# Entry of a hybrid retention and attention block: first attention values from x without its norm, and two value groups as seven products of block sums

## The chip, the cores and the metric

The kernel runs on one core of one Trainium2 chip. The metric is the device time of one execution in microseconds (us). Before the change three executions took 2205.68, 2205.74 and 2206.14 us, a median of 2205.74.

The core has a matrix engine (PE, with its weight loads shown apart as PEld), a vector engine (DVE), an activation engine (ACT), a general engine (POOL) and SP, which here only issues transfers. Each works through its own queue in order. ACT and POOL can issue transfers too. Matrix products are accumulated in PSUM (eight banks), which PE writes and DVE and ACT read. Everything else lies in SBUF.

## The reference, cut to what matters

```python
mod = jax.nn.silu(c) @ w_ada[l] + b_ada[l]
sh1, sc1, g1, sh2, sc2, g2 = jnp.split(mod, 6, axis=-1)
h = modulate(rms_norm(x, norm1_g[l]), sh1, sc1)      # rms_norm * (1 + sc1) + sh1
...
proj = h @ w_in
parts = jnp.split(proj, IN_OFFSETS, axis=-1)
...
for gi, (win, dil) in enumerate(ATT_GROUPS):
    aq, ak, av = parts[4 + 3 * gi], parts[5 + 3 * gi], parts[6 + 3 * gi]
```

Sequence and width are 1024. The three attention values `av` are each 1024 x 512 with 1024 summed over. Only they and the making of `h` are touched.

The norm divides a row of x by its root mean square, so each row has one factor (rstd). Writing a for g(1 + sc1), a value row is rstd times (x·a) times W, plus sh1 times W. The last part is the same for every row. This identity is what the change uses.

## The kernel before, in words

All products are float32 results made of two rounded halves: an operand t is split into `hi` (rounded, written by ACT) and `lo` (the rest, written by DVE), and a product is hi·hi + hi·lo + lo·hi, three matmuls. x is held transposed in eight column blocks `xt[k]` of 128 x 1024; `hh[k]` and `hl[k]` are the halves of h.

The entry (`startup`, L401) loads x by rows (`xn`, eight blocks of 512 KB), squares it on ACT for rstd, loads the scale and shift weights `em` and `xt`, and computes the modulation columns on DVE (`mod1`, L458: one multiply with a running sum per 128 columns). `rstd_bcast` spreads rstd over the partitions with four small float32 matmuls for each half. For every k, `h1_mods`, `h1_scale` and `h1_low` make h: DVE multiplies by a and rstd, ACT adds the shift and rounds, DVE forms the low half.

`av_k` (L796) then does values: for group g and column k, 8 row chunks by 3 matmuls of 512 columns into eight PSUM banks. Group 0 follows h column by column (`av_first`); groups 1 and 2 (`av_step`) follow once h is complete. That is 3 groups x 8 x 8 x 3 = 576 matmuls. At the end of a group ACT empties the eight banks and SP writes them to DRAM (`va_d`, L817 and L818). While groups 1 and 2 run, `sums_of_h` prepares the block sums t1, t2 and t3 of h for the next stage, and SP carries the bias rows through DRAM (`bias_out`, L451).

Next comes `queries_keys` (L1007), whose pairs of projections already use seven products of 2 x 2 block sums for eight (`Blocks`), with the same t1 to t4. Its first matmul is the first row named `qap`.

The order of the queues is written out by hand: the program's order is each engine's order. A tile pool has a fixed number of buffers (26 for `x`, three each for `wh` and `wl`), and an instruction that fills one waits for the last reader of what lay there.

Of the kernel before, what the change touches and what calls it, by code (L numbers as in the profile page):

```python
# [11 lines left out]
F32 = mybir.dt.float32  # L12
# [5 lines left out]
P = 128  # L18
D = 1024
# [121 lines left out]
def block_kernel(ctx, tc, io, stop=None, dbg=None):  # L141
# [205 lines left out]
    xt = [x4(f"xt{k}") for k in range(NK)]  # L347
    rb1 = x4("rb1")
# [6 lines left out]
    def early_load(k):  # L355

        for i in (SC1 + k, SH1 + k):
            early[i] = x4(f"em{i}")
            nc.sync.dma_start(early[i], io["w_ada"][i])
        nc.sync.dma_start(xt[k], io["xT"][k])  # L360
# [33 lines left out]
    ss1 = xpool.tile([P, NK], F32, name="ss1")  # L394
    first = {"lows": []}

# [4 lines left out]
    def startup(issue, prepare, limits):  # L401
        limits = iter(limits)
        first["release"] = lambda: issue(next(limits))
        crow, orow = x4("crow")[:1], x4("orow")[:1, :P]
        nc.vector.memset(rel[32:33], 1.0)
        nc.vector.memset(orow, 1.0)
        nc.sync.dma_start(crow, io["c"])

        xn = [x4(f"xn{b}") for b in range(NC)]
        for b in range(NC):  # L410
            nc.sync.dma_start(xn[b], io["x"][b])
            if b == 1:
                nc.sync.dma_start(rel[:32], io["rel_bias"])
                for g in range(3):
                    nc.sync.dma_start(bias_cut(onehot, g)[:33], io["onehot"][:, 384 * g:384 * g + 384])
            if b == 4:
                nc.sync.dma_start(ct, io["cst"])
                nc.sync.dma_start(vec, io["vec"])
        for k in range(NK):
            early_load(k)  # L420
            if k in (0, 1, 3):
                issue((k + 3) // 2)
        for j in range(2):
            pc = ps_s(f"pc{j}")
            nc.tensor.matmul(pc, orow, crow[:, j * 512:(j + 1) * 512], start=True, stop=True)
            nc.scalar.activation(cb[:, j * 512:(j + 1) * 512], pc, AF.Silu)
        for b in range(NC):
            nc.scalar.activation(xn[b], xn[b], AF.Square, accum_out=ss1[:, b:b + 1])
        for g in range(3):
            bias_rows(g)  # L430
        rs = rstd_of(ss1, "n1", xpool)
        mod1(0)
        nc.vector.tensor_scalar_add(bs1, vec[:, VC_BADA + SC1:VC_BADA + SC1 + NK], 1.0)
        h1_mods(0)
        first["rb"] = [rstd_bcast(rs, 4 * j, 4, f"n1{j}") for j in range(2)]
        prepare(1)
        for j in range(2):
            h1_scale(0, j)
        mod1(1, (SC1,))
        h1_low(0)  # L440
        first["lows"].pop(0)()
        mod1(1, (SH1,))
# [32 lines left out]

    def h1_mods(k):
        sh = mods[:, SH1 + k:SH1 + k + 1]
        nc.vector.tensor_add(sh, sh, vec[:, VC_BADA + SH1 + k:VC_BADA + SH1 + k + 1])
        nc.vector.scalar_tensor_tensor(a1[:, k:k + 1], mods[:, SC1 + k:SC1 + k + 1], bs1[:, k:k + 1],
                                       vec[:, VC_N1 + k:VC_N1 + k + 1], op0=ALU.add, op1=ALU.mult)  # L480

    def h1_scale(k, j=None):

        ts = slice(0, S) if j is None else slice(512 * j, 512 * j + 512)
        t = xt[k][:, ts]
        nc.vector.scalar_tensor_tensor(t, t, a1[:, k:k + 1], rb1 if j is None else first["rb"][j],
                                       op0=ALU.mult, op1=ALU.mult)
        nc.scalar.activation(hh[k][:, ts], t, AF.Identity, bias=mods[:, SH1 + k:SH1 + k + 1])

    def h1_low(k):  # L490
        nc.vector.scalar_tensor_tensor(hl[k], xt[k], mods[:, SH1 + k:SH1 + k + 1], fv(hh[k]),
                                       op0=ALU.add, op1=ALU.subtract)
# [301 lines left out]
    av = {}  # L794

    def av_k(g, k, w):  # L796

        ws = slice((k % 2) * 512, (k % 2) * 512 + 512)
        if k == 0:
            av[g] = [ps_s(f"av{g}{c}") for c in range(NC)]  # L800
        if g == 0:

            parts = ((hh, 0), (hl, 0), (hh, 1)) if k == 0 else ((hh, 1), (hh, 0), (hl, 0))
            groups = (parts[:1], parts[1:2], parts[2:]) if k == 0 else (parts[:2], parts[2:])
        else:
            parts = ((hh, 1), (hh, 0), (hl, 0))
            groups = (parts,)
        for group in groups:
            for c in range(NC):
                for x, j in group:  # L810
                    nc.tensor.matmul(av[g][c], x[k][:, c * C:(c + 1) * C], w[j][:, ws], start=k == 0 and (x, j) == parts[0],
                                     stop=k == NK - 1 and (x, j) == parts[2], skip_group_check=True)
        for c in range(NC) if k == NK - 1 else ():
            if c % 2 == 0:
                t = x4(f"avo{g}{c}")
            o = t[:, DV * (c % 2):DV * (c % 2) + DV]
            nc.scalar.copy(o, av[g][c])  # L817
            nc.sync.dma_start(va_d[g][c * C:(c + 1) * C], o)  # L818

    def split_first(raw):  # L820
        hi = whl.tile([P, 1024], F32R, tag="wh", name=raw.name + "h")
        lo = whl.tile([P, 1024], F32R, tag="wl", name=raw.name + "l")
        nc.scalar.copy(hi, raw)
        first["lows"].append(lambda: nc.vector.tensor_sub(lo, raw, fv(hi)))
        return hi, lo

    split_first.weight = True

    def av_first(kk):

        def body(ahead, w):
            for k in (2 * kk, 2 * kk + 1):
                if k == 0:
                    for j, rb in enumerate(first["rb"]):
                        nc.scalar.copy(rb1[:, 512 * j:512 * j + 512], rb)
                if k % 2 == 0:
                    ahead(1)
                if k + 1 < NK:
                    h1_mods(k + 1)
                    h1_scale(k + 1)  # L840

                    if first["lows"]:
                        first["lows"].pop(0)()
                        h1_low(k + 1)
                        if k + 2 < NK:
                            mod1(k + 2)
                    elif k + 2 < NK:
                        mod1(k + 2, (SC1,))
                        h1_low(k + 1)
                        mod1(k + 2, (SH1,))  # L850
                    else:
                        h1_low(k + 1)
                av_k(0, k, w)
                if k == 3:
                    first["release"]()
                if k == 4:
                    for g in range(3):
                        bias_out(g)
                if k == NK - 1:
                    ahead(1)  # L860
                    if first["lows"]:
                        first["lows"].pop(0)()
                    nc.sync.dma_start(cs, io["cossin"])
                    nc.sync.dma_start(decay, io["decay"])
        return body
# [8 lines left out]
    def sums_of_h(name, ms=range(4)):  # L874

        low = None
        for m in ms:
# [4 lines left out]
            if name == "t1":  # L882
                r = e0
                nc.vector.tensor_sub(r, e0, e1)
            elif name == "t3":
                r = e1
                nc.vector.scalar_tensor_tensor(r, e1, dsh1[:, m:m + 1], o1, op0=ALU.add, op1=ALU.subtract)
            elif name == "t2":
                r = o1
                nc.vector.scalar_tensor_tensor(r, o1, sh, e0, op0=ALU.add, op1=ALU.add)  # L890
            else:
                r = o0
                nc.vector.scalar_tensor_tensor(r, o0, sh, o1, op0=ALU.add, op1=ALU.subtract)
# [3 lines left out]
            if low:  # L897
                nc.vector.tensor_sub(low[0], low[1], fv(low[2]))
            hi, lo = XA[name, m]
            nc.scalar.copy(hi, r)  # L900
            low = lo, r, hi
        nc.vector.tensor_sub(low[0], low[1], fv(low[2]))

    def av_step(g, kk):
        def body(w):
            if (g, kk) == (1, 0):
                for m in range(4):
                    nc.sync.dma_start(h12_d[m][:, 0], fv(hh[2 * m][:, 512:]))
                    nc.sync.dma_start(h12_d[m][:, 1], fv(hl[2 * m][:, 512:]))
                sh = mods[:, SH1:SH1 + NK].rearrange("p (m j) -> p m j", j=2)  # L910
                nc.vector.tensor_sub(dsh1, sh[:, :, 0], sh[:, :, 1])
            for k in (2 * kk, 2 * kk + 1):
                av_k(g, k, w)
            if g == 1 and kk < 3:
                sums_of_h(("t1", "t3", "t2")[kk])
# [1665 lines left out]
```

## Time and profile before

| what | value |
|---|---|
| median of three runs | 2205.74 us |
| span of the profiled execution, first to last instruction | 2203.6 us |
| around the span, by the median | 2.1 us |
| PE busy in the span | 2170.7 us (99%) |
| DVE, ACT, POOL busy | 1456.9, 922.9, 160.6 us |
| DRAM read, written | 316.27 MB, 156.13 MB |

The profiled execution has no time of its own beside its span. A row of the timeline reads: start, duration, engine, line of the code, operation, result and operands, and in brackets the idle time before it with what ended it. `128x512` is partitions by elements. A row of the groups has the busy time of the group and the mean of one instruction in ns after the bar. PE rows overlap, because matmuls are pipelined: the rate is the distance from start to start.

### The profile page before, as it was taken

What the parts mean: (1) busy time and instruction counts of PE and PEld (TensorE: products, weight loads), DVE (VectorE), ACT (ScalarE), POOL (GpSimd) and SP (SyncE); (2) the same over time, 40 slices, a digit from 0 to 9 for tenths busy, and PEclk for the clock granted to TensorE, in tenths of its full rate; (3) what the DMA queues carried; (4) which work ended last, traced back from release to release, by engine and by line L of the source; (5) the groups of instructions that cost most, each with busy time, mean ns of one, the idle gap of its engine ahead of it and who ended that gap; (6) DMA issues with size and microseconds to landing.
All of it is one profiled execution on the core that took longest, in us unless ns stands there. A gap on an engine that the chain in (4) does not pass through costs nothing. (4 is left out here: it accounts for less than half of the span.)

```text
span 2203.6 us, 27246 instructions
## 1 busy us (share of the span) xinstructions
PE 2170.7 (99%) x10134; PEld 1802.4 (82%) x10134; DVE 1456.9 (66%) x2284; ACT 922.9 (42%) x1691; POOL 160.6 (7%) x192
## 2 busy tenths in 40 slices
PE   7999999999999999999999999999999999999998
PEld 4888888888887888888888888888778888888887
DVE  6618777763547778865564754677876665887855
ACT  4323332223334445444554634524455445533413
POOL 0001111000011122111100000001100000000003
PEclk9999999999999999999999999999999999999999
DMA  9539999634676556557863265654144344745322
GB/s 367 202 128 284 304 289 292 193 115 172 233 267 209 166 179 220 177 161 197 195 173 97 87 244 186 239 179 160 62 166 152 146 149 177 262 136 175 119 86 77
DMA packets 156611, 408.93 MB, mean 186 GB/s; under 512 B 27446, under 2 KB 55357, under 8 KB 153278
## 3 DMA queue, kind: packets, MB, share of 16 engines
q1 hardware_dynamic: 148542, 363.14, 46.8%
q0 software_dynamic: 7936, 44.05, 9.2%
q8 instruction: 80, 1.31, 0.2%
q14 instruction: 53, 0.43, 0.1%
HBM read 316.27 MB, written 156.13 MB: 214 GB/s over the span
## 5 line engine op out<-in xcount | busy, mean ns | idle before, releaser
L207 PE MATMUL qap<-hh,qaw 128*128 128x512 f32 x216 | 84.0, 389 | 0.0
L209 PE MATMUL qap<-hl,qaw 128*128 128x512 f32 x216 | 84.0, 389 | 0.0
L211 PE MATMUL qap<-hh,qaw 128*128 128x512 f32 x216 | 84.0, 389 | 0.0
L638 POOL TENSOR_TENSOR j<-qk,j 128x512 fp32r<-128x512 f32 x32 | 43.3, 1353 | 458.3 <-ACT j L637 441.7
L1902 POOL TENSOR_TENSOR accnf<-accnf,sqnf 128x256 f32<-128x256 f32 (+1 forms) x18 | 16.6, 922 | 609.6 <-ACT sqnf L1898 609.6
L2006 ACT ACTIVATE a<-a 128x512 f32<-128x512 f32 x48 | 30.3, 631 | 73.3 <-DVE a L2005 73.3
L1322 ACT ACTIVATE P<-P,ng 128x128 f32<-128x128 f32 (+1 forms) x96 | 42.0, 439 | 37.5 <-DVE ng L1319 37.5
L264 DVE TENSOR_TENSOR qaw<-wa,qaw 128x512 fp32r<-128x512 f32 x54 | 36.0, 685 | 30.4 <-ACT qaw L254 30.4
L2214 ACT CAST w2h<-w2s 128x512 fp32r<-128x512 f32 x36 | 22.4, 622 | 80.0 <-DVE w2s L2252 78.8
L264 DVE TENSOR_TENSOR fw<-w1r,fw 128x512 fp32r<-128x512 f32 x48 | 32.9, 688 | 33.6 <-ACT fw L254 33.6
L207 PE MATMUL fp<-h2h,fw 128*128 128x512 f32 x128 | 50.0, 391 | 0.0
L211 PE MATMUL fp<-h2h,fw 128*128 128x512 f32 x128 | 49.8, 389 | 0.0
L209 PE MATMUL fp<-h2l,fw 128*128 128x512 f32 x128 | 49.8, 389 | 0.0
L207 PE MATMUL roa<-rh,rwl 128*128 128x512 f32 x128 | 49.8, 389 | 0.0
L209 PE MATMUL roa<-rl,rwh 128*128 128x512 f32 x128 | 49.8, 389 | 0.0
L211 PE MATMUL roa<-rh,rwh 128*128 128x512 f32 x128 | 49.8, 389 | 0.0
L1737 DVE TENSOR_TENSOR rwl<-rwl,rwh 128x1024 fp32r<-128x1024 f32 x25 | 30.2, 1221 | 29.0 <-ACT rwh L1767 29.0
L673 ACT COPY sm<-sT 128x128 f32<-128x128 f32 x32 | 8.5, 267 | 93.8 <-PE sT L661 93.8
L207 PEld LDWEIGHTS qap<-hh,qaw 128*128 128x128 f32 x216 | 40.6, 188 | 8.5
L211 PEld LDWEIGHTS qap<-hh,qaw 128*128 128x128 f32 x216 | 40.6, 188 | 8.4
L209 PEld LDWEIGHTS qap<-hl,qaw 128*128 128x128 f32 x216 | 40.6, 188 | 8.4
L1902 POOL TENSOR_TENSOR accn<-accn,sqn 128x512 f32<-128x512 f32 x12 | 15.5, 1293 | 392.2 <-ACT sqn L1898 392.2
(3104 smaller groups left out, 7211.6 us busy)
## 6 DMA issues: line engine op xcount, KB each, us to landing
v<-vd SPq DMA_DIRECT2D x32, 512.0 KB, 5.0
raw<-in_w_ada_dram SPq DMA_DIRECT2D x32, 512.0 KB, 5.0
w1r<-in_w_ff_dram SPq DMA_DIRECT2D x32, 512.0 KB, 4.8
vd<-vo SPq DMA_DIRECT2D x24, 512.0 KB, 6.4
yt<-y POOLq DMA_DIRECT2D x24, 512.0 KB, 6.9
xsd<-as SPq DMA_DIRECT2D x24, 512.0 KB, 2.7
w2r<-in_w_ff2s_dram SPq DMA_DIRECT2D x24, 512.0 KB, 7.2
em<-in_w_ada_dram SPq DMA_DIRECT2D x16, 512.0 KB, 10.2
```

The costliest lines, as they stand in the source:

```text
L207: nc.tensor.matmul(o, wl, xh, start=first, stop=False, skip_group_check=skip)
L209: nc.tensor.matmul(o, wh, xl, start=False, stop=False, skip_group_check=skip)
L211: nc.tensor.matmul(o, wh, xh, start=False, stop=last, skip_group_check=skip)
L264: nc.vector.tensor_sub(t[:, 512:], src, fv(t[:, :512]))
L638: nc.gpsimd.tensor_sub(t[:, 1], src, fv(t[:, 0]))
L673: nc.scalar.copy(sm, ps[:, :C])
L1322: nc.scalar.activation(v, v, AF.Exp, bias=ng[:, blk:blk + 1], accum_out=st[:, g, blk, 2 + a:3 + a])
L1737: nc.vector.tensor_sub(lo, fv(lo), fv(hi))
L1902: (nc.vector if f == 7 else nc.gpsimd).tensor_add(G["acc", key], G["acc", key], sq)
L2006: nc.scalar.activation(o, o, AF.Relu)
L2214: nc.scalar.copy(hi, src)
```

## The change

Four things are exchanged:

- **Group 0 without rstd and shift.** The products run on x·a, split without the norm (`plain_split`, `plain_low`). rstd is computed on the side, stored to DRAM (`rs_d`) and read back in two layouts: spread over all partitions (`rb1`) and one factor for each row (`rsn`). ACT multiplies by `rsn` when it empties a bank. The shift's part is made by POOL from the raw weights (`shift_rows`, `shift_sum`), summed over the partitions by two float32 matmuls with ones (`shift_out`), and added to `va_d[0]` in DRAM by four accumulating transfers.
- **h later.** `h_scale` and `h_split` make the true h from `xt` after the plain products, half by half, where the seven products need it.
- **Groups 1 and 2 as seven products.** Their 1024 x 1024 weight lies as blocks in DRAM (`w_av2`). `UPLAN` names the seven products, each 4 row chunks x 4 x 3 = 48 matmuls of 512 columns. POOL adds the weight blocks (`u_sum`), ACT and DVE split them (`u_w`), and `u_post` adds the seven results.
- **Loads.** `c` is read spread over the partitions in place of a matmul; small tables go through the queues of ACT and POOL. The order of loads is one list, drawn by `more`. The low halves of the group 0 weights 1 to 3 and of the first product move from DVE to POOL.

The diff, cut to its core:

```diff
+    def plain_split(k, ts):
+        nc.scalar.mul(hh[k][:, ts], xt[k][:, ts], a1[:, k:k + 1])
+    def plain_low(k):
+        nc.vector.scalar_tensor_tensor(hl[k], xt[k], a1[:, k:k + 1], fv(hh[k]), op0=ALU.mult, op1=ALU.subtract)
+    def h_scale(k, j):
+        t = xt[k][:, 512 * j:512 * j + 512]
+        nc.vector.scalar_tensor_tensor(t, t, a1[:, k:k + 1], rb1[0][:, 512 * j:512 * j + 512],
+                                       op0=ALU.mult, op1=ALU.mult)
+    def h_split(k, j):
+        ts, sh = slice(512 * j, 512 * j + 512), mods[:, SH1 + k:SH1 + k + 1]
+        t, hi, lo = xt[k][:, ts], hh[k][:, ts], hl[k][:, ts]
+        nc.scalar.activation(hi, t, AF.Identity, bias=sh)
+        late_low(lambda: nc.vector.scalar_tensor_tensor(lo, t, sh, fv(hi), op0=ALU.add, op1=ALU.subtract))
...
+    def wa_split(kk, parts=(slice(0, 1024),)):
...
+            nc.scalar.copy(hi[:, cs_], raw[:, cs_])
+            if kk > 0:
+                nc.gpsimd.tensor_sub(lo[:, cs_], raw[:, cs_], fv(hi[:, cs_]))
...
+            if k == 5:
+                rs = rstd_of(ss1, "n1", xpool)
+                rb1.append(x4("rb1"))
+                nc.gpsimd.dma_start(rs_d.rearrange("o (p b) -> (o p) b", b=NC), rs)
+                nc.gpsimd.dma_start(rb1[0], rs_d.to_broadcast([P, S]))
+                for j in (0, 4):
+                    src = bass.AP(tensor=rs_d.tensor, offset=rs_d.offset + P * j, ap=[[1, P], [P, 4]])
+                    nc.gpsimd.dma_start(rsn[:, j:j + 4], src)
+            if k + 1 < NK:
+                scale_mod(k + 1)
+                for ts in (H0, H1):
+                    plain_split(k + 1, ts)
+                if k % 2 == 1:
+                    wa_split((k + 1) // 2)
+                plain_low(k + 1)
...
+            if k == 6:
+                for m in range(4):
+                    h_scale(2 * m, 0)
+                    h_split(2 * m, 0)
+                u_w(0, 0, "pool")
+                u_w(0, 1, "pool")
+                late_low()
+        for c in range(NC):
+            mms(NK - 1, [(hh, 1), (hh, 0), (hl, 0)], [c])
...
+            nc.scalar.mul(o, av[c], rsn[:, c:c + 1])
+            nc.sync.dma_start(va_d[0][c * C:(c + 1) * C], o)
...
+    UPLAN = {"11": ("11", 1, "a"), "12": ("21", 1, "b"), "s1": ("t1", 1, "c"), "s2": ("t2", -1, "a"),
+             "s4": ("22", 1, "c"), "s3": ("t3", -1, "a"), "22": ("t4", -1, "a")}
...
+    def more_values(ahead):
...
+            if i == 0:
+                u_load(1)
+            if n == "11":
+                u_w(1, 0)
+                u_w(1, 1)
+                for m in range(4):
+                    u_mm(0, 0, [m])
+                    u_mm(0, 1, [m])
+                    u_mm(0, 2, [m])
+                    u_mm(0, 3, [m])
+                    for k in range(2 * m + 1, 2 * m + 2):
+                        shift_mod(k)
+                        h_scale(k, 0)
+                        h_split(k, 0)
+                        shift_rows(k - 1)
+                late_low()
+                u_load(2)
...
+                for m in range(4):
+                    h_scale(2 * m, 1)
+                u_sum(2)
+                for k in (1, 3, 5, 7):
+                    shift_rows(k)
+                for kk in (1, 2, 3):
+                    shift_sum(kk)
+                for g in range(3):
+                    bias_out(g)
+                continue
+            for p in range(4):
+                u_mm(i, p)
+                if post:
+                    u_post(*post.pop())
+                post.append((i, p))
+                if p == 0 and n[0] != "2" and USEQ[i + 1][0] == "s" and i > 1:
+                    u_sum(i + 1)
+                if p == 1 and i + 2 <= last:
+                    u_load(i + 2)
+                if n == "12":
+                    sums_of_h("t1", [p])
+                    if p > 1:
+                        u_w(2, p - 2)
...
+                elif n == "s3":
+                    sums_of_h("t4", [p])
+                    if p > 1:
+                        u_w(6, p - 2)
+                    if p == 3:
+                        late_low()
+                        shift_out()
```

In the parts left out, product `s1` is accompanied by t2 and the weights of `s2`, `s2` by the second halves of h (`h_split`) and the weights of `s4`, and `s4` by t3 and the weights of `s3`. `late_low` holds back one low half, so that it is formed behind the next instruction's start. The fourth sum t4, made within `queries_keys` before, is made in `s3`.

More of the change, by code (lines that the diff above doesn't have):

```diff
@@ L419, in startup @@
[L419 to L442, printed above, removed]
+    def late_low(f=None):
+        if first["lows"]:
+            first["lows"].pop()()
+        if f:
+            first["lows"].append(f)
@@ L820, in split_first @@
[L820 to L865, printed above, removed]
@@ new lines, in u_load @@
+    def u_load(i):
+        n = USEQ[i]
+        for j in range(2):
+            if n in ("s1", "s3"):
+                U["sum", n == "s3", j] = t = x4(f"usum{i}{j}")
+                u_raw(t, "21", j)
+        for j in range(2):
+            if i == 0:
+                U["more", i, j] = x4(f"uraw{j}")
+            else:
+                U["more", i, j] = whl.tile([P, 1024], F32, tag=("wh", "wl")[j], name=f"um{i}{j}")
+            u_raw(U["more", i, j], {"s1": "22", "s2": "11", "s4": "12", "s3": "11"}.get(n, n), j)
@@ new lines, in shift_rows, with shift_sum, shift_out @@
+    def shift_rows(k):
+        t = wa[k // 2][0][:, 512 * (k % 2):512 * (k % 2) + 512]
+        nc.gpsimd.tensor_scalar_mul(t, t, mods[:, SH1 + k:SH1 + k + 1])
+    def shift_sum(kk):
+        nc.gpsimd.tensor_add(wa[0][0], wa[0][0], wa[kk][0])
+    def shift_out():
+        ps = ps_s("shw")
+        for j in range(2):
+            nc.tensor.matmul(ps, ones.to_broadcast([P, P]), wa[0][0][:, 512 * j:512 * j + 512], start=j == 0, stop=j == 1)
+        t = x4("shw")
+        for j in range(2):
+            nc.scalar.copy(t[:, 512 * j:512 * j + 512], ps)
+        for i in range(4):
+            dst = va_d[0][2 * C * i:2 * C * (i + 1)].rearrange("(a p) x -> p a x", p=P)
+            nc.gpsimd.dma_start(dst, t.rearrange("p (a x) -> p a x", a=2), accum_op=ALU.add)
@@ L1154, in values @@
         banks(False)
-    for kk in range(4):
-        steps.add(av_first(kk), [(io["w_av"][kk], split_first)], manual=True)
-    for g in (1, 2):
-        for kk in range(4):
-            steps.add(av_step(g, kk), [(io["w_av"][4 * g + kk], split_first if (g, kk) == (1, 0) else split_w)])
-    steps.mark()
+    steps.add(first_values, manual=True)
+    steps.add(more_values, manual=True)
     steps.add(queries_keys, manual=True)
```

292 lines of the change are left out of this document (202 added, 90 removed).

## The prediction

> **What bounds the kernel now.** I read the page's totals first, then the waits of PE in the first 320 us, then three windows cut where the stages change, then the timeline at the cuts.
>
> ```profile
> span 2203.6 us, 27246 instructions
> PE 2170.7 (99%) x10134; PEld 1802.4 (82%) x10134; DVE 1456.9 (66%) x2284; ACT 922.9 (42%) x1691; POOL 160.6 (7%) x192
> ...
> PE n10rb L387 <- POOL n1rs L380: 8.6, 1, 8.6
> PE av L811 <- ACT hh L488: 3.5, 5, 1.2
> ...
> 0.00:23.17 23.17, 11.40 (x26) 5.32 (x26) 3.88 (x11) 14.08 (x24) 2.78 (x5) 1.00 0.92 350
> 23.17:74.80 51.63, 48.01 (x203) 37.62 (x203) 43.66 (x63) 17.25 (x22) 0.00 (x0) 1.00 0.75 282
> 74.80:159.60 84.80, 84.80 (x375) 70.23 (x375) 28.44 (x39) 25.50 (x38) 0.00 (x0) 1.00 0.45 161
> ...
> 149.64 0.39 PE L811 MATMUL av<-raw_880h,hh 128*128 128x512 f32 x1
> ...
> 159.39 0.39 PE L811 MATMUL av<-raw_880h,hl 128*128 128x512 f32 x1
> 159.62 0.39 PE L207 MATMUL qap<-hh,qaw 128*128 128x512 f32 x1
> ```
>
> PE sets the time: 99% busy, with no wait behind the entry. The entry waits for rstd (8.6 us) and for h (3.5 us), and the first value product starts at 23.17 us. In the third window PE never rests, while DVE is busy for 28.44 of 84.80 us (columns: length, then busy PE, PEld, DVE, ACT, POOL) and POOL not at all. The 43 steps from 149.64 to 159.39 give 0.227 us per matmul. The first `qap` at 159.62 us is my mark: behind it PE is full, so whatever the mark moves by, the end moves by.
>
> **What the change takes from PE.** Seven products are 7 x 48 = 336 matmuls against 384 for two groups: 48 x 0.227 = 10.9 us less. `shift_out` adds two plain float32 products of 512 columns:
>
> ```profile
> 21.38 1.91 PE L387 MATMUL n11rb<-ct,n1rs 128*128 128x128 f32 x8
> ```
>
> Four products of 128 columns (eight records) took 1.9 us, so two of 512 cost 3.6 us. Group 0 can start near 11 us, 12 us sooner, since it waits for c, one scale block, one x block and half a weight, not for all of x. If PE never waited, 63 us for the end of group 0, 336 matmuls (76.3) and 3.6 would put the mark near 143 us, 16.7 us early. The question is what feeds PE.
>
> **What the change loads on DVE and POOL.** Durations, and how these two meet:
>
> ```profile
> L463 DVE SCALAR_TENSOR_TENSOR em<-em,cb 128x1024 f32<-128x1024 f32 x16 | 19.3, 1220 | 0.0
> 33.96 1.22 DVE L463 SCALAR_TENSOR_TENSOR em<-em,cb 128x1024 f32<-128x1024 f32 x1
> 35.22 0.16 DVE L478 TENSOR_TENSOR mods<-mods,vec 128x1 f32<-128x1 f32 x1
> 35.30 0.21 DVE L479 SCALAR_TENSOR_TENSOR a<-mods,bs,vec 128x1 f32<-128x1 f32 x1
> 162.57 1.41 DVE L893 SCALAR_TENSOR_TENSOR xt<-xt,mods 128x512 f32<-128x512 f32 x2
> 676.59 1.29 DVE L764 TENSOR_TENSOR statel<-state,stateh 128x512 fp32r<-128x512 f32 x2
> L1902 POOL TENSOR_TENSOR accn<-accn,sqn 128x512 f32<-128x512 f32 x12 | 15.5, 1293 | 392.2 <-ACT sqn L1898 392.2
> L1902 POOL TENSOR_TENSOR accnf<-accnf,sqnf 128x256 f32<-128x256 f32 x12 | 8.8, 737 | 15.4 <-ACT sqnf L1898 15.4
> ...
> 639.72 1.29 POOL L638 TENSOR_TENSOR j<-qk,j 128x512 fp32r<-128x512 f32 x1 [0.30 <-ACT j L637]
> 639.77 2.31 DVE L1072 TENSOR_TENSOR vwl<-vwl,vwh 128x1024 fp32r<-128x1024 f32 x1
> 1485.33 1.29 POOL L1902 TENSOR_TENSOR accn<-accn,sqn 128x512 f32<-128x512 f32 x1 [342.84 <-ACT sqn L1898]
> 1486.23 1.48 DVE L198 TENSOR_TENSOR raw_12332l<-raw,raw_12332h 128x1024 fp32r<-128x1024 f32 x1 [1.64 <-ACT raw_12332h L197]
> 2157.18 1.29 POOL L1902 TENSOR_TENSOR accnf<-accnf,sqnf 128x512 f32<-128x512 f32 x1 [2.62 <-ACT sqnf L1898]
> 2157.21 0.75 DVE L2369 SCALAR_TENSOR_TENSOR x1r<-f2l,mods,x1r 128x512 f32<-128x512 f32 x1 [0.84 <-PE f2l L211]
> ```
>
> From start to start DVE needs 1.15 us for 1024 columns, 0.7 for the three-operand form of 512 and 0.64 for the plain one; a modulation column with its addition costs 1.3 (33.96 to 35.30). POOL's two sizes differ by 0.55 us per 256 columns, so 1024 columns should take 2.4 us.
>
> The pairs of rows at 639 and 1485 us matter most. A DVE operation that alone takes 1.2 us took 2.31 and ended at 642.08, which is 1.07 behind POOL's end at 641.01; the other ended at 1487.71, 1.09 behind POOL's 1486.62. DVE stood still until POOL was done. Both its operands lay in SBUF. At 2157.21 one operand (`f2l`) lay in PSUM, and DVE ran at its usual 0.75 beside POOL. So I count POOL's time onto DVE's wherever DVE reads two SBUF operands.
>
> All collisions in this trace are of the plain two-operand form. About 35 us of DVE's new work behind group 0 (counted below) is the three-operand form, which shift columns, scales, low halves of h and three of the sums use. The nearest row says that the place of the operands decides, so I take it to collide as well; the bounds are no collision and the whole of POOL's time.
>
> The Trainium skill's page "SBUF — State Buffer", section "Who interferes with whom", states this generally: a DVE instruction with two SBUF inputs shares a read interface with any POOL instruction that reads SBUF, and the second to start waits for the first to end. By that rule the three-operand form collides too and the sum stays as below; by the plain form alone it would be the second rival's.
>
> **The chain, step by step.**
>
> ```profile
> 12.86 1.06 ACT L428 ACTIVATE xn<-xn 128x1024 f32<-128x1024 f32 x1 [0.84 <-DMA xn<-in_x_dram]
> 14.15 1.06 ACT L428 ACTIVATE xn<-xn 128x1024 f32<-128x1024 f32 x1
> 22.40 0.72 ACT L488 ACTIVATE hh<-xt,mods 128x512 fp32r<-128x512 f32 x1 [0.79 <-DVE xt L486]
> 25.69 1.05 ACT L823 CAST raw_315h<-raw 128x1024 fp32r<-128x1024 f32 x1
> 71.19 4.01 ACT L817 COPY avo<-av 128x512 f32<-128x512 f32 x8 [4.41 <-PE av L811]
> 75.23 6.70 SPq L818 DMA_DIRECT2D vad<-avo  x8
> raw<-in_w_ada_dram SPq DMA_DIRECT2D x32, 512.0 KB, 5.0
> L380 POOL TENSOR_TENSOR n1rs<-n1rs,ct 128x8 f32<-128x8 f32 x1 | 2.6, 2572 | 16.4 <-DVE n1rs L379 16.4
> 651.11 0.54 POOL L1145 DMA_DIRECT2D hl<-h12d  x1 [4.88 <-issue]
> ```
>
> *To the end of group 0.* A block of 512 KB lands every 1.3 us (12.86, 14.15; the former is x's sixth, so the first lands by 6.4). Column 7's x is the 29th in the new list: 43 us. Scale column, two ACT pieces (0.72 each) and low half add 4.1; with POOL's weight difference in the way DVE is through column 7 at about 48.5. Four shift columns (5.2), four scales and four lows (5.6) and the collision with POOL's third weight difference (2.4) bring it to 61.7. That difference stands in POOL's queue behind the power (2.6), three issues of the rstd transfers and their wait; the small-element read of `rsn` is unknown, between nothing and the 4.9 us that one transfer waited at 651.11. It can hold PE before column 6, so group 0 ends between 63 and 67. This is cover: nothing below hangs on it, since DVE is later.
>
> *The gate.* ACT's queue has the halves of h, then the first product's two weight casts (2 x 1.05), then the eight evictions (4.0): it empties the first bank at 63 and the last at 67. SP's eight stores last 6.7 us as before, to 70.3, and only behind them does SP issue the load of the second product's weights. Landing (5.0) and cast (1.05) make 76.4. In DVE's queue that weight's low half stands ahead of the four odd shift columns and all that follows, so DVE idles from 62 to 76, though nothing else keeps it. POOL's first low halves and even shift rows fall into that gap and cost nothing.
>
> *From 76.4 on DVE and POOL in a row.* DVE: product `11`: two weight lows 2.3, four shift columns 5.2, four scales and four lows 5.6, four more scales 2.8 = 15.9. `12`: t1 (8 x 0.64), two weight lows 2.3, three posts 2.1, four scales 2.8 = 12.3. `s1`: 8.4 (a post, t2, weight lows). `s2`: eight lows, four sums, weight lows 10.7. `s4`: three posts, t3, weight lows 9.8. Together 57.1. POOL: four `u_sum` of two adds 19.2; odd shift rows 4 x 0.9 (one operand; between half and all of the 1.29 above) 3.6; three `shift_sum` 7.2. Together 30.0. The seven posts read PSUM and could run beside POOL (4.9); I credit half, 2.5. The last low half for `s3` is then made at 76.4 + 57.1 + 30.0 - 2.5 = 161.0.
>
> PE needs only 44 us for `12` to `s4`, so it waits at every stage; the first wait, in the first row chunk of `12`, is over 10 us by itself (PE is through `11` near 77, the last odd low half comes near 95). Behind 161.0 PE has most of `s3` (9.3), `shift_out` (3.6) and `22` (10.9): mark at **184.8 instead of 159.6, 25 us later**. The span becomes 2228.8. The median lies 2.1 us above the span now, and I keep that: **2231 us**, 1.1% slower.
>
> The remaining edits go together at nothing: t4 moved out of the queries stage, `a_load` moved behind the values, the bias rows on SP and the copy of h to DRAM. All are covered by PE's full queue there; the bias rows occupy SP some 19 us, and the next weights are needed later than that:
>
> ```profile
> 55.40 0.39 SPq L453 DMA_DIRECT2D browd<-rows  x1
> ...
> 71.85 2.39 SPq L456 DMA_DIRECT2D biasd<-browd  x4
> ```
>
> **The rivals.**
>
> *No collision to speak of (not slower).* If DVE runs its three-operand forms freely and POOL takes the gaps, only the gate at 76.4 and PE remain: `12`'s first chunk ends 13.1 + 0.7 later at 90.2, then 8.2 for its rest, five products (54.5), 3.6 and some 3 us of late weight lows: mark at 159.6, time 2206. It decides from the point where less than a tenth of POOL's 30 us reaches DVE. With stores as fast as the evictions the gate is 2.7 earlier: 2203. For it speaks that no three-operand collision is in this trace; against it the two pairs of rows.
>
> *Half a collision.* Only plain forms wait, or POOL finds DVE waiting for ACT half the time: 15 us less, 2216.
>
> *More waits.* The rstd transfers (4-byte pieces on POOL's queue) or tile buffers hold the evictions by 7 us, and POOL's eleven additions take 3.0 us each, 6.6 more: 2245. The 4.88 us wait speaks for it.
>
> *The start does not move:* if the plain products began no sooner than 23 us, DVE would be 12 us later throughout: 2243. The order of loads speaks against it.
>
> **How the numbers follow.** Forecast (2222 to 2240) 0.50; half a collision 0.19; more waits 0.12; the start 0.02; no collision 0.17. A run of this kernel tells 0.2%, 4.4 us, from no change: 2201.3 to 2210.2 is the same. No collision is split between same and faster, since gate and evictions can be some us earlier: faster 0.08, same 0.09, and slower 0.83 for the rest. The range 2205 to 2247 leaves out the faster part of no collision and the far end of more waits.
>
> **What would show it.** Right: first `av` product near 11 us; DVE idle for over 10 us ahead of the second product's weight low; PE waiting for DVE in `12`, `s1`, `s2` and `s3`; DVE rows of the three-operand form at 512 columns lasting 2 to 3 us beside POOL rows of 2.4; the first `qap` near 185. Wrong: such rows at 0.75 beside POOL, or a PE without waits behind 95 us.

## The result, and the profile after

Four executions of the changed kernel took 2233.91 to 2236.72 us, a median of 2235.55; four of the kernel before beside them had a median of 2205.84. The ratio is 1.0135, with a 95% interval of 1.0120 to 1.0149: about 30 us slower. The profiled execution took 2236.72 us with a span of 2234.9, 31.3 above the span before.

The page's totals:

```profile
span 2234.9 us, 27298 instructions
PE 2172.3 (97%) x10070; PEld 1799.1 (80%) x10070; DVE 1508.1 (67%) x2320; ACT 939.6 (42%) x1720; POOL 226.6 (10%) x225
```

PE's waits in the first 260 us (us in all, times, longest):

```profile
PE av L847 <- POOL wv3wl L801: 12.9, 1, 12.9
PE ub L207 <- DVE hl L438: 10.4, 3, 7.8
...
PE uc L209 <- DVE uwl L939: 4.9, 4, 2.4
PE qap L207 <- DVE qat L293: 3.8, 1, 3.8
PE uc L207 <- ACT uwh L934: 3.5, 1, 3.5
```

And the line of the instructions on `qap` whose first start I had taken as the mark (shortest, median and longest ns, then first and last start):

```profile
L207 PE MATMUL qap<-hh,qaw x216: 389/389/795, 184.3 to 530.5; 128*128 128x512 f32 x108
```

The mark lies at 184.3 us, 24.7 later than before. The span grew by 31.3, so 6.6 us were lost behind the mark.

The entry in the windows that answer to those of before (length, then busy PE, PEld, DVE, ACT, POOL with their instructions, then the granted clock, the DMA share and GB/s), with one window behind the mark:

```profile
23.17:74.80 51.63, 38.76 (x161) 31.52 (x160) 31.30 (x42) 26.62 (x42) 21.05 (x13) 0.87 0.72 282
74.80:160.00 85.20, 64.17 (x236) 48.59 (x235) 77.65 (x80) 30.25 (x47) 41.99 (x17) 0.84 0.52 180
...
220.00:230.00 10.00, 8.68 (x28) 6.95 (x29) 9.71 (x16) 3.28 (x6) 0.52 (x1) 0.68 0.72 204
```

In the third window DVE went from 28.44 to 77.65 us of about 85, POOL from nothing to 41.99, and PE, which was full, issued 236 matmuls up to 160.00 where it had issued 375 up to 159.60. The clock fell too, which it had not done before.

The places in the timeline that carry the chain, in order of time:

```profile
11.96 3.78 PE L847 MATMUL av<-wv0wh,hh 128*128 128x512 f32 x8 [1.36 <-ACT hh L412]
...
57.47 0.77 POOL L861 DMA_DIRECT2D rsn<-rsd  x1 [6.96 <-issue]
58.23 2.94 DVE L438 SCALAR_TENSOR_TENSOR hl<-xt,mods,hh 128x512 fp32r<-128x512 f32 x1
58.25 2.35 POOL L801 TENSOR_TENSOR wv3wl<-wv,wv3wh 128x1024 fp32r<-128x1024 f32 x1
60.66 0.79 PE L847 MATMUL av<-wv3wl,hh 128*128 128x512 f32 x1 [12.87 <-POOL wv3wl L801]
61.75 0.74 DVE L438 SCALAR_TENSOR_TENSOR hl<-xt,mods,hh 128x512 fp32r<-128x512 f32 x1
...
69.54 5.45 ACT L893 ACTIVATE avo<-av,rsn 128x512 f32<-128x512 f32 x8 [2.40 <-PE av L847]
70.26 5.08 SPq L894 DMA_DIRECT2D vad<-avo  x8
74.10 0.39 PE L207 MATMUL ua<-uwh,hl 128*128 128x512 f32 x1
75.44 1.99 SPq L906 DMA_DIRECT2D um<-in_w_av_dram  x2
80.07 1.06 ACT L934 ACTIVATE uwh<-um 128x1024 fp32r<-128x1024 f32 x1 [5.07 <-DMA um<-in_w_av_dram]
81.22 1.23 DVE L939 TENSOR_TENSOR uwl<-um,uwh 128x1024 fp32r<-128x1024 f32 x1 [12.00 <-ACT uwh L934]
...
99.92 9.13 DVE L430 SCALAR_TENSOR_TENSOR xt<-xt,a,rb 128x512 f32<-128x512 f32 x4
100.22 8.27 POOL L983 TENSOR_TENSOR wv<-wv,wv 128x1024 f32<-128x1024 f32 x3
...
116.44 2.75 POOL L926 TENSOR_TENSOR usum<-usum,um 128x1024 f32<-128x1024 f32 x1 [7.94 <-DVE uwl L939]
116.88 3.40 DVE L939 TENSOR_TENSOR uwl<-usum,uwh 128x1024 fp32r<-128x1024 f32 x1
...
160.96 1.23 DVE L941 SCALAR_TENSOR_TENSOR uwl<-usum,uwh 128x1024 fp32r<-128x1024 f32 x1
```

The same DVE form lasts 2.94 us at 58.23 and 0.74 at 61.75; beside the first stands a POOL operation that ends at 60.60. Four scales take 9.13 us beside three POOL additions. DVE waits 12.00 us for the second product's weight, whose load SP issues at 75.44, behind eight stores that wait for the evictions, which wait for PE, which waited 12.87 us for a POOL operation behind the transfers of rstd. The first `ua`, at 74.10, is the first matmul behind group 0.

What was lost behind the mark, POOL's and ACT's timeline:

```profile
175.05 1.29 POOL L995 DMA_DIRECT2D vad<-shw  x1 [31.00 <-ACT shw L992]
181.45 1.23 POOL L995 DMA_DIRECT2D vad<-shw  x1 [5.11 <-issue]
187.94 1.21 POOL L995 DMA_DIRECT2D vad<-shw  x1 [5.25 <-issue]
202.73 1.19 POOL L995 DMA_DIRECT2D vad<-shw  x1 [13.59 <-issue]
...
210.37 0.62 ACT L254 CAST qaw1s<-qas 128x512 fp32r<-128x512 f32 x1 [8.39 <-DMA vad<-shw]
211.93 0.58 ACT L286 COPY qat<-qap 128x512 f32<-128x512 f32 x1
...
221.32 0.80 PE L207 MATMUL qap<-hh,qaw 128*128 128x512 f32 x1 [3.82 <-DVE qat L293]
```

The four accumulating transfers of the shift read a tile of the `x` ring and go out slowly. The cast of a later weight into that ring waits 8.39 us for them, and behind it in ACT's queue stands the copy `qat` that PE needs. PE stands for 3.8 us, and then its clock is 0.68 over 10 us, which is worth up to another 3.2 (an estimate: 0.32 of 10 us).

### The profile page after: what moved, and what is told of

It reads as the page before. It is cut to its first block, busy times and chain, and to the rows that moved or that the text cites. A ratio compares the mean times of both kernels' runs of the same rounds, so it can differ in the third digit from the quotient of the medians.

```text
span 2234.9 us, 27298 instructions
## 1 busy us (share of the span) xinstructions
PE 2172.3 (97%) x10070; PEld 1799.1 (80%) x10070; DVE 1508.1 (67%) x2320; ACT 939.6 (42%) x1720; POOL 226.6 (10%) x225
## 5 line engine op out<-in xcount | busy, mean ns | idle before, releaser
L2199 ACT ACTIVATE a<-a 128x512 f32<-128x512 f32 x48 | 30.3, 631 | 73.6 <-DVE a L2198 73.6
L207 PEld LDWEIGHTS qap<-hh,qaw 128*128 128x128 f32 x216 | 41.1, 190 | 12.9 <-DVE qat L293 4.2
L2200 ACT ACTIVATE a<-a 128x512 f32<-128x512 f32 x64 | 40.5, 632 | 2.0
```

The source lines that it names most:

```text
L207: nc.tensor.matmul(o, wl, xh, start=first, stop=False, skip_group_check=skip)
L2199: nc.scalar.activation(o, o, AF.Relu)
L2200: nc.scalar.activation(o, o, AF.Square)
```

## The experiments

My theory: one chain (late third weight, late evictions, late load, then DVE and POOL in a row) sets the mark, and a DVE operation with two SBUF operands stands still while POOL reads SBUF. The rivals: POOL's work lies in gaps; PE's own late end of group 0 decides; or one of the two waits alone.

Each experiment below except the last pair has one run and one trace. Five kernels that are equal up to the gate (DVE's first row for the second product's weight: the changed one, `pool_add`, `pool_set`, `sums_dve`, `shw_tile`) have it between 80.65 and 82.40 us, so a single difference of marks is good to one or two microseconds.

### Does POOL's time count onto DVE's?

Three additions into a tile that nobody reads any more, behind the shift sums on POOL; and in their place fills of the same tile, which read nothing:

```diff
                     shift_sum(kk)
+                for _ in range(3):                              # pool_add
+                    nc.gpsimd.tensor_add(wa[1][0], wa[2][0], wa[3][0])
+                for _ in range(6):                              # pool_set, instead
+                    nc.gpsimd.memset(wa[1][0], 0.0)
```

> Three more additions of 128 x 1024 on POOL behind the shift sums, over weights that nobody reads any more: 8.3 us of POOL time, placed where POOL idles until 116 us. Theory (the collision): DVE loses nearly all of it, first qap 6 to 8 us later at 190 to 192, time 2241 to 2244. Rival (POOL matters only through what it hands on): nothing waits for these, 184 and 2235.

> At the place of the three extra additions POOL runs six fills of 128 x 1024, which write SBUF and read nothing. Theory (DVE's second SBUF operand and POOL's reads share one way in): no collision, first qap at 184 to 185, time 2235 to 2236. Rival (any POOL instruction stops DVE): the fills' own time, some 3 to 8 us, is lost as with the additions, 187 to 192, time 2239 to 2243.

With the additions the first `qap` came at 192.5 and the run took 2243.88 us: 8.2 later, beside 8.32 us more of POOL. POOL and DVE there:

```profile
109.01 8.32 POOL L1031 TENSOR_TENSOR wv<-wv,wv 128x1024 f32<-128x1024 f32 x3
...
109.53 2.86 DVE L1108 TENSOR_TENSOR xt<-xt 128x512 f32<-128x512 f32 x1
112.31 0.67 DVE L972 TENSOR_TENSOR ur<-ur,ub 128x512 f32<-128x512 f32 x1
112.90 2.23 DVE L1108 TENSOR_TENSOR xt<-xt 128x512 f32<-128x512 f32 x1
115.06 2.83 DVE L1125 TENSOR_TENSOR xat<-xt,xat 128x512 fp32r<-128x512 f32 x1
```

With the fills it came at 183.6 (2235.09 us), no later than in the changed kernel:

```profile
107.87 5.99 POOL L1031 MEMSET wv<- 128x1024 f32 x6
...
108.40 0.68 DVE L1108 TENSOR_TENSOR xt<-xt 128x512 f32<-128x512 f32 x1
109.00 0.67 DVE L972 TENSOR_TENSOR ur<-ur,ub 128x512 f32<-128x512 f32 x1
```

The near match of 8.2 and 8.32 is in part chance. The gate had come 0.57 us later before any addition ran (81.79 for 81.22). The three stretched rows are 5.9 us longer than the 0.68 that they take alone, and 1.8 us more came later, where DVE waited for PE (1.65 us at 163.43). So an addition cost DVE itself about 2 us of its 2.8.

So it is POOL's reading that stops DVE, not that POOL is busy; and `ur`, whose second operand lies in PSUM, keeps its 0.67 us beside an addition too. The Trainium skill's page "SBUF — State Buffer", section "Who interferes with whom", says just this: a DVE instruction with two SBUF inputs contends with a POOL instruction that reads SBUF, not with one that only writes. The two runs agree on each half of it.

### POOL's work taken away

All eight additions of weight blocks go to DVE, which then has more to do:

```diff
-            nc.gpsimd.tensor_add(s, s, U["more", i, j])
+            nc.vector.tensor_add(s, s, U["more", i, j])
```

> The eight additions of weight blocks move from POOL (2.6 to 2.8 us each) to DVE (1.15 each). Theory: POOL's eight cost DVE some 17 us by standing still, its own eight cost 9.2, so first qap some 6 to 9 us earlier at 175 to 178, time 2226 to 2229, though DVE has more to do. Rival (DVE is bound by its own work, POOL runs beside it): 9 us later, 193, time 2244.

The first `qap` came at 176.9 and the run took 2227.35 us: 7.4 earlier, though DVE makes eight operations more and the gate, which the edit does not touch, came 1.2 us later (82.40). Next, the shift rows and sums left out:

```diff
-                        shift_rows(k - 1)
...
-                for k in (1, 3, 5, 7):
-                    shift_rows(k)
-                for kk in (1, 2, 3):
-                    shift_sum(kk)
```

> The eight shift_rows and three shift_sum on POOL are left out, so the shift's part of the group 0 values is not the reference's. Nothing on PE or DVE waits for them before s3. Theory (DVE stands still while POOL reads): the odd rows and the sums lay over a dense DVE from 91 to 108 us, so 12 to 17 us go: first qap at 168 to 172, time 2218 to 2223. Rival (no collision: DVE's own work and the late load bound): under 2 us, 2233 to 2235.

It came at 177.4 (2228.84 us), 6.9 earlier and not 12 to 16. The scales that stood beside the sums went from 9.13 us back to 2.73:

```profile
98.70 2.73 DVE L430 SCALAR_TENSOR_TENSOR xt<-xt,a,rb 128x512 f32<-128x512 f32 x4
```

That is 6.4 of the 6.9. The rows (one operand, 1.55 us each when alone) had run beside short DVE operations and cost little: 6.9 less 6.4 leaves 0.5. My price for the sums (7.2) was about right, the one for the rows (3.6) too high.

### The waits ahead

The second product's load ahead of the eight stores; the odd shift columns ahead of its weight lows in DVE's queue; the reads of rstd from DRAM moved in POOL's queue behind the third weight's difference:

```diff
             nc.scalar.mul(o, av[c], rsn[:, c:c + 1])          # load_first
-            nc.sync.dma_start(va_d[0][c * C:(c + 1) * C], o)
+            outs.append(o)
+        u_load(1)
+        for c, o in enumerate(outs):
+            nc.sync.dma_start(va_d[0][c * C:(c + 1) * C], o)
...
             if n == "11":                                     # odd_first
-                u_w(1, 0)
-                u_w(1, 1)
                 for m in range(4):
...
                         shift_rows(k - 1)
+                u_w(1, 0)
+                u_w(1, 1)
                 late_low()
...
-                nc.gpsimd.dma_start(rb1[0], rs_d.to_broadcast([P, S]))   # wv3_early
-                for j in (0, 4):
-                    src = bass.AP(tensor=rs_d.tensor, offset=rs_d.offset + P * j, ap=[[1, P], [P, 4]])
-                    nc.gpsimd.dma_start(rsn[:, j:j + 4], src)
...
                     wa_split((k + 1) // 2)
+                if k == 5:
+                    nc.gpsimd.dma_start(rb1[0], rs_d.to_broadcast([P, S]))
+                    for j in (0, 4):
+                        src = bass.AP(tensor=rs_d.tensor, offset=rs_d.offset + P * j, ap=[[1, P], [P, 4]])
+                        nc.gpsimd.dma_start(rsn[:, j:j + 4], src)
                 plain_low(k + 1)
```

> The load of the second product's weights is issued ahead of the eight stores of group 0's values, not behind them. Theory (a late load gates DVE, and from there DVE and POOL work as one): the load lands about 5 us sooner (81.2 becomes 76 for the first weight low half), and the first qap moves from 184.3 to about 179; time about 2230. Rival (the clock that PE loses after its waits, or PE's waits for group 0, set the time): no move beyond 1 us, 2235.

> In product 11 the odd columns' shift, scale and halves stand ahead of the second product's weight split in the queues of DVE and ACT. Theory: DVE uses the gap from 69 to 81 us, so 10 to 12 us of the chain go: first qap at 172 to 175, time 2223 to 2226. Rival (POOL's additions and shift rows are the bound by themselves, DVE only waits for them): less than 4 us, since POOL's work is the same: 2231 to 2235.

> The last group 0 weight difference stands ahead of the two readbacks of rstd in POOL's queue. Theory: PE's single wait of 12.9 us before column 6 goes; it was cover for the most part, since DVE's chain starts from the load behind the stores. Evictions begin some 5 us sooner (now they wait for the second readback), so the gate opens 4 to 6 us earlier: first qap at 178 to 181, time 2229 to 2232. Rival (PE's waits are what is lost): the full 12.9 us, 171 to 172, time 2222.

| edit alone | time, us | first `qap`, us | earlier by |
|---|---|---|---|
| load_first | 2234.39 | 181.4 | 2.9 |
| odd_first | 2228.15 | 177.5 | 6.8 |
| wv3_early | 2230.95 | 178.2 | 6.1 |

Loading first moved the low half only from 81.22 to 79.36 us, just outside the spread above, and not to 76. SP still waits for PE's last `av`, whose weights lie in the buffer that the load fills, and issues it at 74.61 where it was 75.44; the second half's cast began at 81.59 where it was 81.57.

```profile
79.36 1.23 DVE L943 TENSOR_TENSOR uwl<-um,uwh 128x1024 fp32r<-128x1024 f32 x1 [10.03 <-ACT uwh L938]
```

Letting DVE do the odd columns in the gap was worth more, but 6.8 us and not the 10 to 12 that I expected. There too DVE meets POOL: the first column's multiply ran into POOL's low halves of the first product (to 71.66) and took 3.42 us where its group's mean before had been 1.22.

```profile
66.46 5.20 POOL L937 TENSOR_TENSOR uwl<-uraw,uwh 128x1024 fp32r<-128x1024 f32 x2 [5.67 <-ACT uwh L934]
...
69.33 3.42 DVE L459 SCALAR_TENSOR_TENSOR em<-em,cb 128x1024 f32<-128x1024 f32 x1
```

With the third weight early, PE's wait of 12.9 us is gone, and 6.1 us of it reach the mark. What I had called cover was a link of the chain.

### Behind the mark

The sum of the shift goes to a tile of 2 KB for each partition, outside the ring:

```diff
+    shw_t = xpool.tile([P, 512], F32, name="shwt")
...
-        t = x4("shw")
-        for j in range(2):
-            nc.scalar.copy(t[:, 512 * j:512 * j + 512], ps)
+        nc.scalar.copy(shw_t, ps)
...
-            nc.gpsimd.dma_start(dst, t.rearrange("p (a x) -> p a x", a=2), accum_op=ALU.add)
+            nc.gpsimd.dma_start(dst, shw_t.rearrange("p (a x) -> p a x", a=1).to_broadcast([P, 2, 512]), accum_op=ALU.add)
```

> The result of shift_out lies in a tile of its own of 128 x 512, read twice by each accumulating transfer, not in one of the 26 shared x tiles. Theory for the 6.6 us that the changed kernel loses behind its first qap: a weight tile of the next stage waits for the shared tile until the fourth transfer ends (PE waits 3.8 us, and then runs at a lower clock for some us). So the first qap stays at 184 and the distance from there to the end falls by 5 to 7 us: time 2229 to 2231. Rival (the next stage's loads stand behind 22 us of stores on SP): no change, 2235.

The cast's wait, PE's wait and the fall of the clock were gone (last `qap` 523.1 in place of 530.5), yet the run took 2235.43 us. The 7 us (0.5 of them lay ahead of the mark) were given back near 690 us, in a wait that the changed kernel does not have. ACT's timeline:

```profile
689.22 0.27 ACT L652 COPY sm<-sT 128x128 f32<-128x128 f32 x1 [8.83 <-DMA vd<-vr]
```

And PE's longest wait from 520 to 720 us:

```profile
PE kv L207 <- DVE kl L666: 5.5, 2, 4.9
```

The changed kernel waits 1.6 us there, and its clock keeps 1.00 where it fell to 0.80 here (690 to 706 us): the last `rg` came at 704.8 beside 705.9, so 6.3 of the 7.4 us were gone. `sm` is the first small tile of the next stage; by that wait, its place had just held a result on its way to DRAM. Taking one tile out of the ring changes which buffer each later tile gets, so I took the order of the ring for the cause and kept it in the last pair.

### All together

The four edits that gained (the load, the odd columns, the third weight, the additions on DVE), and then POOL without any arithmetic on large tiles:

```diff
-                nc.gpsimd.tensor_sub(lo[:, cs_], raw[:, cs_], fv(hi[:, cs_]))       # combo2, on top
+                nc.vector.tensor_sub(lo[:, cs_], raw[:, cs_], fv(hi[:, cs_]))
-                u_w(0, 0, "pool")
-                u_w(0, 1, "pool")
+                u_w(0, 0)
+                u_w(0, 1)
-        nc.gpsimd.tensor_scalar_mul(t, t, mods[:, SH1 + k:SH1 + k + 1])
+        nc.scalar.mul(t, t, mods[:, SH1 + k:SH1 + k + 1])
-        nc.gpsimd.tensor_add(wa[0][0], wa[0][0], wa[kk][0])
+        nc.vector.tensor_add(wa[0][0], wa[0][0], wa[kk][0])
```

> Four of the single edits at once: the second product's weights loaded ahead of the stores, odd shift columns ahead of its weight lows, the rstd transfers issued earlier in POOL's queue, and the eight weight-block additions on DVE. Alone they brought the first qap from 184.3 to 181.4, 177.5, 178.2 and 176.9. Theory (late load, late third weight and collisions with POOL are separate links of one chain, so the gains nearly add): 184.3 - 23.2 = 161.1, so qap at 160 to 165 and a time of 2211 to 2217. Rival (DVE's time in a row is one and the same gap, which each edit shortens until the next holder appears): no more than about twice the largest gain, qap at 169 to 172, time 2220 to 2224. DVE's row of the second product's first weight low should begin by 74 instead of 81.2 by either.

> The same four edits, and POOL does no arithmetic on SBUF tiles behind the power any more: the low halves of the weights go to DVE (five at 1.2 us), the three shift sums to DVE (three at 1.2), the eight shift rows to ACT. That adds 9.6 us to DVE and takes some 10 (weight lows), 12 (rows) and 8 us (sums) off POOL, which DVE waited for in part. Theory (POOL's time counts onto DVE's): qap 5 to 10 us earlier than with the four edits alone, 152 to 158 if those give 161, time 2202 to 2209, and no DVE row of 1024 columns above 1.5 us between 20 and 150 us. Rival (DVE is simply full, and what comes on top of it costs): qap no earlier than with the four edits, or up to 5 us later.

The four gains nearly add: together 22.2 of their sum of 23.2 (first `qap` at 162.1, 2213.25 us). That is what separate links of one chain give; the rival had 169 to 172. The second product's low half began at 78.95 and not by 74, because DVE had the odd columns to finish first. Without POOL's arithmetic no DVE row of 1024 columns between 20 and 150 us lasted over 1.5 us, and the mark came at 156.8, ahead of the 159.6 before the change; but the run took 2209.53 us beside 2205.44, because the loss behind the mark was still there:

```profile
182.72 0.62 ACT L254 CAST qaw1s<-qas 128x512 fp32r<-128x512 f32 x1 [8.25 <-DMA vad<-shw]
```

The last pair, eleven runs each: the tile of its own, with the ring tile kept for one copy so that the ring keeps its order; and, on top of it, the sums of `s1` and `s3` made by accumulating loads:

```diff
         t = x4("shw")                                         # own_place
-        for j in range(2):
-            nc.scalar.copy(t[:, 512 * j:512 * j + 512], ps)
+        nc.scalar.copy(t[:, :512], ps)
+        nc.scalar.copy(shw_t, t[:, :512])
...
+        if n in ("s1", "s3"):                                 # dma_sums, on top, in u_load
+            for j in range(2):
+                blk = {"s1": 3, "s3": 0}[n]
+                nc.gpsimd.dma_start(U["sum", n == "s3", j], io["w_av2"][blk, j], accum_op=ALU.add)
+            return
```

> The kernel without POOL arithmetic and with the four other edits, and besides the four accumulating transfers of the shift read a 2 KB tile of their own, to which ACT copies the sum, so that the ring of x tiles keeps its order and no tile of it waits for these transfers. The version before it had its first qap at 156.8, 2.8 us ahead of the kernel before the change, and still took 4.1 us longer, so 6.9 us are lost behind the mark. Theory (all of that is the weight cast that waits for a tile which the fourth transfer holds, and the clock that falls behind PE's wait): qap at 157 to 158, no PE wait for qat, granted clock 1.00 from 170 to 220, and a time 6.9 us lower, 2202 to 2204 against 2205.5 before the change. Rival (as with the own tile in the changed kernel alone, the gain is given back at the values' end near 655 us, or elsewhere behind): 2208 to 2210, with a PE wait that is not in the profile of before.

> The same, and four of the eight weight-block additions (those of s1 and s3, whose two blocks both come from DRAM) are made by accumulating transfers on POOL's queue in place of DVE. DVE loses 4 x 1.2 = 4.8 us of the stretch from 57 to 135 us that it fills without a pause. Theory (DVE is what bounds this stretch now, and its work counts one for one): qap at 152 to 153.5, time 2197 to 2199.5, 0.3% under the kernel before the change. Rival (each accumulating transfer costs POOL's queue 5 to 14 us, as the four of the shift did, so the sums of s1 come later than the 93 us at which ACT casts them, or those of s3 later than 130): DVE waits there for 5 us and more, qap at 157 to 165, time 2203 to 2211.

The kernel with the tile of its own has its mark at 157.2, no wait for `qat`, a granted clock of 1.00 from 170 to 220 us, and at the retention stage the waits of before (1.0 and 0.6). It took 2202.80 us (2201.61 to 2204.51, 11 runs) beside 2205.65: a ratio of 0.9987 with an interval of 0.9978 to 0.9996. That is 1.5% below the changed kernel and 0.13% below the kernel before: less than the 0.2% that I had called the same, but the whole interval lies below 1. With the ring's order kept the gain stayed, which fits the explanation of the wait at `sm`; the own tile without the ring tile was not run on this version.

The accumulating loads gained nothing: mark 157.3, time 2204.29 us (2201.71 to 2205.28, 11 runs), ratio 0.9992 (0.9984 to 1.0001). The median is 1.5 us above that of the kernel without them, and the ranges overlap. DVE's busy time from 57 to 135 us fell from 75.12 to 70.88, and the sums of `s1` were early enough. In place of the work came waits for the second block of `s2`, which SP issued at 94.98, and PE waited for its cast:

```profile
101.60 1.23 DVE L939 TENSOR_TENSOR usum<-usum,um 128x1024 f32<-128x1024 f32 x1 [3.58 <-DMA um<-in_w_av_dram]
...
108.76 0.50 PE L207 MATMUL ua<-uwh,xat 128*128 128x512 f32 x1 [3.15 <-ACT uwh L947]
```

The time lies in my rival's range, but not for its reason, and neither of my two cases had named that load. What it would be worth to issue it earlier was not tried.

## Why the prediction was right, and where it was not

*The direction and most of the size.* The forecast was 2231 us with the mark at 184.8; it was 2235.55 with the mark at 184.3. But the mark came out so close because errors of both signs met.

*What the change takes from PE* held: the first product began at 11.96 us (I had some 11).

*The end of group 0*: I had the first bank ready at 63 and the last at 67. ACT began to empty them at 69.54, and PE's last `av` came just ahead of 74.10. POOL's queue held the third weight, and with it PE, to 60.60. "This is cover: nothing below hangs on it, since DVE is later" was the wrong step. The evictions, the stores and the load that DVE then waited for hang on the end of group 0, so the gate itself was late, at 81.2 and not 76.4. Taking PE's wait away earned 6.1 us of mark.

*The gate* was right as a mechanism: 12.00 us of DVE waiting, with nothing else that kept it, and 6.8 us back when its own work was put ahead. Its place was 4.8 us too early.

*DVE and POOL in a row* was right as a mechanism, and is the one step that was shown from both sides: additions put in move the mark, fills do not, and additions taken away bring it back. The stretch from the gate to the last low half took 161.0 - 76.4 = 84.6 us in the forecast and 162.1 - 81.2 = 80.9 on the chip (the next row of DVE starts at 162.10). POOL's terms were each too dear. Taking every DVE row there that lasted longer than its form does alone, I estimate that POOL cost DVE 25 us: the eight additions 17.1 (forecast 19.2), the three sums 6.4 (7.2), the odd shift rows 1.5 at most (3.6). I had 30.0, less 2.5 of credit. POOL's rows themselves were longer than forecast (22.0 us for the eight), so not all of a POOL row is lost on DVE. `sums_dve` bears this out: 17.1 less 9.2 for DVE's own eight additions is 7.9, and it gained 7.4 of mark, 8.6 from its own gate on. From there to the mark I had 23.8, and it took 22.2. Against +4.8 at the gate stand -3.7 and -1.6: the sum is -0.5, by luck.

*"The remaining edits go together at nothing"* failed, and is 6.6 of the 31.3 us of span. I had named PE's full queue as their cover and looked at SP's time; I did not ask which tile the accumulating transfers hold and who gets it next. The transfers were four lines of the diff. With a tile of its own and the ring's order kept, 6.7 us came back (2209.53 to 2202.80).

*The rivals.* No collision and half a collision fall with these 25 us, where they had nothing and 15. "More waits" had the right place, the transfers of rstd: one was held 6.96 us in POOL's queue. Its price, 6.1 us of mark where I wrote 7, came in another way: through PE and so the evictions' start, not through an operand of the evictions.

## What to carry to other kernels

When an engine takes over work, ask first which operand reads it shares with the engine that is about to become the bound: POOL's eight additions cost DVE about 17 us here, and the kernel got faster when DVE made them itself, in about 9. Work called cover has to be followed to the end of its queue, because an eviction, its store and a load behind it can be what the covered engine waits for. And a slow transfer may cost nothing in the queue that issues it, but its tile goes back to a ring, and the next owner pays.

## What was not expected of the hardware

The granted clock fell where PE had waited for some microseconds, and matmuls then took up to twice as long for a while: 0.79 us for the one behind the 12.87 us wait (0.39 is usual), 0.80 behind 3.82 us. In the kernel with the tile of its own, two waits did it and a short one did not:

```profile
64.22 0.80 PE L207 MATMUL ua<-uwh,hl 128*128 128x512 f32 x1 [5.52 <-ACT avo L896]
93.20 0.80 PE L207 MATMUL uc<-uwh,xat 128*128 128x512 f32 x1 [4.15 <-ACT uwh L940]
109.35 0.50 PE L209 MATMUL ua<-uwl,xat 128*128 128x512 f32 x1 [0.69 <-DVE uwl L947]
```

Its windows (the granted clock stands behind the five engines) show 0.66 around the first two and 1.00 around the third:

```profile
60.00:70.00 10.00, 5.78 (x15) 4.64 (x16) 9.53 (x16) 9.40 (x16) 0.00 (x0) 0.66 0.77 284
90.00:100.00 10.00, 5.49 (x12) 4.02 (x13) 9.91 (x15) 3.58 (x5) 0.00 (x0) 0.66 0.66 185
...
105.00:120.00 15.00, 14.23 (x62) 11.10 (x61) 14.86 (x20) 12.99 (x21) 0.00 (x0) 1.00 0.75 268
```

The Trainium skill's page "TensorE: Matmul & The Clock Gate", section "What's actually happening", gives half rate after an idle window of about 3.4 us and full rate again after a busy one; these rows agree with it. Other rows here show that a shorter wait can do it too. In `shw_tile`, with a wait of 1.06 us just before, it took 2.26 us, and the fall came 1.3 us later:

```profile
135.23 0.51 PE L209 MATMUL ua<-uwl,xat 128*128 128x512 f32 x1 [2.26 <-DVE uwl L942]
...
136.86 0.63 PE L209 MATMUL ua<-uwl,xat 128*128 128x512 f32 x1
```

In `load_first` the same two waits (1.07 and 2.26 us, to 132.78) were followed by matmuls of 0.39 to 0.40 only, so the length of the waits alone does not decide it. Behind the mark, a wait of 3.8 us cost 6.6 us in the changed kernel, and one of 3.0 us cost 4.6 in `sums_dve` (span less mark, against the kernel before). I had priced PE's waits at their length alone.

The other surprise was how slowly the accumulating transfers leave POOL's queue: 5.11, 5.25 and 13.59 us from the end of one issue to the next between 176 and 203 us, in each case put down to the issue itself. What holds them was not found.
